# Mixer: the first four heads' attention in two steps with transposes two projected tiles later, and the mLSTM norm's gain as a scale of ScalarE's copies

## The chip, the cores and the metric

The kernel runs on one core of one Trainium2 chip. The metric is the device time of one execution in microseconds (us); of the kernel before there are three runs, with a median of 2618.13 us. One of its executions was recorded by the hardware profiler.

The engines are called by the profile's names: PE (TensorE; PEld is its weight load), DVE (VectorE), ACT (ScalarE), POOL (GpSimd) and SP (the queue that issues most transfers). Each works through its own instructions in order.

## What is computed

One layer of a diffusion backbone over 256 latent and 256 context tokens, width 2048: a half-step FFN, a mixer, a second half-step FFN. The change lies in the mixer, whose normed input `h` is projected by one wide matrix and split:

```
aq, ak, av, mqk, mv, mo, gt = split(h @ w_in)
att = softmax(rope(norm(aq)) @ rope(norm(ak)).T / sqrt(128)) @ av     # 8 heads, 2 key/value heads
hm  = bidirectional mLSTM(mqk, mv, gt)                                # 8 heads of 128
hm  = rms_norm(hm, m_gain) * sigmoid(mo)                              # m_gain: 8 x 128
out = concatenate([att, hm]) @ w_out
```

## The kernel before

All large products are made in three fp32r matmuls: each operand is split into a high and a low part (`split`, L117: ACT copies `hi`, L125; DVE subtracts for `lo`, L126), and `mm3` (L147 to L149) adds hi*hi, hi*lo and lo*hi in PSUM. A weight piece of 1 MB (`raw`, three buffers) is loaded by SP and split into two halves of `hi` and `lo` (four buffers each).

`project(name, n, toks, bs)` multiplies the latents' two token tiles with 512 columns in 16 steps of one k-tile; a step is 2 x 3 matmuls of 128x512 and is called a **projected tile** here. After each step it yields, and the caller may put other work there. So the order on PE is written out by hand: in the loops over `project("w_o1")` and `project("w_q1")` the step number n decides which generator advances: `o_steps` (sigmoid of the output gate into `gm`), `att[0]` (attention of the first four heads), `outs` (norm and gating of `hm`), `cats` (transposes of `hm`). At the end of every step `project` also advances `beside["part"]`: DVE multiplies a 512 KB piece of the modulation weights, already in `sr` (three buffers, loaded by SP, L287), with the condition vector (L205). In w_o1 and w_q1 that is about 1.2 us of DVE per piece, and a buffer is loaded again when its piece is done. The places of all other engines' instructions follow from a scheduler that lists each engine's instructions once, when the program is built.

`attention(kv)` goes over eight items (two query tiles by four heads). Its i-th step does three things:

- item i: scores (3 matmuls), row maximum `nm` (DVE, L1684, L1685), exponential `pr` with its sum `sd` (ACT, L1688), reciprocal (DVE, L1689), scaling of `pr` (ACT, L1690)
- item i-1: four transposes of `pr` on PE (L1696), copied to `pT` (ACT, L1698)
- item i-2: the products of `pT` with the values on PE (L1705)

Called A(i), T(i-1) and V(i-2) here, they stood at one place: steps n = 2, 8, 11, 14 of w_o1 and 2, 5, 8, 11, 14 of w_q1, and the last behind w_q1. T(i) was thus issued with A(i+1), three projected tiles after A(i) (six for i = 0, four for i = 3). Transposes, whether of `pr` or of `hm`, take turns in two PSUM banks (`tr`).

The mLSTM's gain: `m_gain` is loaded once, repeated over all partitions, into `mg` (L1671, SP; its buffer is that of `C1`, which the last mLSTM products, L1523, read). `ev_o` takes the sigmoid into `gm` (ACT, L1625), and POOL multiplies `mg` onto it (L1626). `mlstm_out` multiplies `hm` by `gm` (DVE, L1727) and by the norm's factor (L1728); `mlstm_cat` transposes the 128x128 blocks of `hm` (PE, L1739), and ACT copies each token tile's four blocks at once into `cx` (128x512, L1741).

## Time and profile before

| | |
|---|---|
| runs before (three) | 2616.05, 2618.13, 2618.64 us; median 2618.13 |
| the profiled execution: span, first to last instruction | 2616.0 us |
| the same: what lies around the span | not given; the median is 2.1 us above the span |
| mean granted TensorE clock | 0.998 |
| busy: PE, PEld, DVE, ACT, POOL | 99%, 83%, 80%, 53%, 8% of the span |
| w_o1 and w_q1, steps n = 0 to 15 each | about 1724 to 1790 us in the span |

A row of the timeline gives start, duration, engine, line, operation, and at its end in brackets the idle time of the engine before it with what ended it. Matmuls overlap: one lasts 0.39 us in the row, but the next starts 0.23 us later, so lost time is read from the starts.

### The profile page before, as it was taken

The page shows a single profiled execution, that of the slowest core. Times are in us where ns is not written, and L with a number is a line of the kernel's source. Part 1 is how long each engine was busy: PE and PEld are TensorE (multiplying, and loading weights), DVE is VectorE, ACT ScalarE, POOL GpSimd, SP SyncE. Part 2 cuts the span into 40 slices and gives each one's busy share as a digit, 9 for nine tenths or more (in the row PEclk, how much of TensorE's full clock was granted, in tenths as well). Part 3 has the DMA queues.
Part 4 walks back from the last instruction along what each step waited for, and adds up shares of the span by engine and source line. Part 5 has one row for each costly group of instructions (what it writes and reads, how often), then busy time and mean ns, then how long its engine had stood idle before and what let it go on. Part 6 is the DMA issues. An engine that isn't in the chain of part 4 may idle for free.

```text
span 2616.0 us, 33774 instructions
## 1 busy us (share of the span) xinstructions
PE 2593.1 (99%) x12742; PEld 2159.5 (83%) x12742; DVE 2099.3 (80%) x2792; ACT 1393.4 (53%) x1798; POOL 208.8 (8%) x261
## 2 busy tenths in 40 slices
PE   8999999999999999999999999999999999999998
PEld 5788888888888888888889889878898888888887
DVE  7788888878888788888886889788887676767767
ACT  5455444444444565444454367557576655555554
POOL 0000010100010100000110000220000000000001
PEclk9999999999999999999999999999999999999999
DMA  9889999999999988889986877777769897988875
GB/s 399 347 213 267 281 267 281 256 275 276 277 274 281 265 248 236 226 214 229 230 243 262 311 272 253 240 245 270 248 231 299 261 252 253 253 248 257 242 225 175
DMA packets 126932, 678.93 MB, mean 260 GB/s; under 512 B 14120, under 2 KB 16680, under 8 KB 64944
## 3 DMA queue, kind: packets, MB, share of 16 engines
q1 hardware_dynamic: 99408, 499.54, 51.4%
q0 software_dynamic: 27360, 177.22, 34.9%
q8 instruction: 100, 1.64, 0.2%
q14 instruction: 64, 0.52, 0.1%
HBM read 658.82 MB, written 17.89 MB: 259 GB/s over the span
## 4 chain that ended last, share of the span: by engine, by line
PE 92%; DVE 3%; DMA 3%; issue 1%; ACT 1%; POOL 0%; SPq 0%; ACTq 0%; POOLq 0%; DVEq 0%
PE mm L147 24%; PE mm L149 24%; PE mm L148 24%; PE mm L85 2%; PE tr L148 2%; PE tr L149 2%; PE tr L147 2%; PE Y L149 1%; PE Y L148 1%; PE Y L147 1%; DMA mraw<-in_w_m 1%; PE X L147 1%; PE X L149 1%; PE X L148 1%; PE tr L85 1%; DVE lo L126 1%
## 5 line engine op out<-in xcount | busy, mean ns | idle before, releaser
L125 ACT ACTIVATE hi<-raw 128x1024 fp32r<-128x1024 f32 (+3 forms) x536 | 556.5, 1042 | 579.6 <-PE mm L149 448.8
L126 DVE TENSOR_TENSOR lo<-raw,hi 128x1024 fp32r<-128x1024 f32 (+1 forms) x524 | 630.1, 1208 | 288.2 <-ACT hi L125 268.8
L125 ACT ACTIVATE hi<-chain 128x1024 fp32r<-128x1024 f32 x320 | 338.1, 1060 | 257.3 <-PE mm L149 150.1
L126 DVE TENSOR_TENSOR lo<-chain,hi 128x1024 fp32r<-128x1024 f32 x320 | 386.8, 1221 | 84.4 <-ACT hi L125 80.0
L147 PE MATMUL mm<-hi,hhi 128*128 128x512 f32 (+3 forms) x1024 | 394.6, 385 | 0.0
L148 PE MATMUL mm<-lo,hhi 128*128 128x512 f32 (+3 forms) x1024 | 387.6, 379 | 0.0
L149 PE MATMUL mm<-hi,hlo 128*128 128x512 f32 (+3 forms) x1024 | 387.3, 378 | 0.0
L205 DVE SCALAR_TENSOR_TENSOR junk<-sraw,cBh 128x1024 fp8e5<-128x1024 f32 x192 | 234.4, 1221 | 26.0 <-DMA sraw<-in_w_mt 23.7
L149 PEld LDWEIGHTS mm<-hi,hlo 128*128 128x128 f32 x1024 | 192.9, 188 | 34.0
L147 PEld LDWEIGHTS mm<-hi,hhi 128*128 128x128 f32 x1024 | 192.9, 188 | 31.4
L148 PEld LDWEIGHTS mm<-lo,hhi 128*128 128x128 f32 x1024 | 193.2, 189 | 30.7
L149 PE MATMUL mm<-hi,hid2l 128*128 128x512 f32 x352 | 137.4, 390 | 0.0
L147 PE MATMUL mm<-hi,hid2h 128*128 128x512 f32 x352 | 137.2, 390 | 0.0
L148 PE MATMUL mm<-lo,hid2h 128*128 128x512 f32 x352 | 137.1, 389 | 0.0
L148 PE MATMUL mm<-lo,h2hi 128*128 128x512 f32 x320 | 124.9, 390 | 0.1
L147 PE MATMUL mm<-hi,h2hi 128*128 128x512 f32 x320 | 124.9, 390 | 0.0
L149 PE MATMUL mm<-hi,h2lo 128*128 128x512 f32 x320 | 124.6, 389 | 0.0
L205 DVE SCALAR_TENSOR_TENSOR sr<-sr,cBl 128x1024 f32<-128x1024 f32 x85 | 102.8, 1219 | 14.7 <-DMA sr<-in_w_mt 14.4
L728 POOL DMA_DIRECT2D chain<-in_w_up1b x60 | 53.0, 884 | 725.3 <-DVE lo L126 698.4
L147 PE MATMUL mm<-hhi,hi 128*128 128x512 f32 (+1 forms) x288 | 101.2, 351 | 0.0
L149 PE MATMUL mm<-hhi,lo 128*128 128x512 f32 (+1 forms) x288 | 98.9, 343 | 0.0
L148 PE MATMUL mm<-hlo,hi 128*128 128x512 f32 (+1 forms) x288 | 98.9, 343 | 0.0
(514 smaller groups left out, 5456.3 us busy)
## 6 DMA issues: line engine op xcount, KB each, us to landing
raw<-in_w_dn SPq DMA_DIRECT2D x70, 1024.0 KB, 7.0
chain<-in_w_up1b POOLq DMA_DIRECT2D x60, 1024.0 KB, 10.5
raw<-in_w_up2b SPq DMA_DIRECT2D x50, 1024.0 KB, 5.7
sraw<-in_w_mt SPq DMA_DIRECT2D x96, 512.0 KB, 8.7
sr<-in_w_mt SPq DMA_DIRECT2D x82, 512.0 KB, 5.3
raw<-in_w_up1b SPq DMA_DIRECT2D x40, 1024.0 KB, 8.1
mraw<-in_w_m SPq DMA_DIRECT2D x32, 1024.0 KB, 7.6
chain<-in_w_dn POOLq DMA_DIRECT2D x30, 1024.0 KB, 8.6
```

What stands on the lines that cost most here:

```text
L85: ins = getattr(self.engine, name)(*a, **k)
L125: scalar[0].activation(hi, src, AF.Copy)
L126: vector[0].tensor_tensor(lo, src, hi.bitcast(F32), op=ALU.subtract)
L147: tensor[0].matmul(out_ap, sh, mh, start=first, stop=False, skip_group_check=skip)
L148: tensor[0].matmul(out_ap, sh, ml, start=False, stop=False, skip_group_check=skip)
L149: tensor[0].matmul(out_ap, sl, mh, start=False, stop=last, skip_group_check=skip)
L205: ins = nc.vector.scalar_tensor_tensor(junk() if junk else raw, raw, 1.0, cB[s], op0=ALU.mult, op1=ALU.mult, accum_out=mT[:, i, s, kt, h : ...
L728: accum = lambda dst, src: nc.gpsimd.dma_start(dst, src, accum_op=ALU.add)
```

## The change

1. `attention(kv, apart=False)`: with `apart` it yields between A(i) and T(i-1). `att[0]` is built with it, so T and V have places of their own. In w_o1 the steps are now n = 2 (two), 8, 10, 11, 13, 14; in w_q1 n = 0, 2, 4, 5, 7, 8, 10, 11, 13, 14 (two). The scores stay at 2, 8, 11, 14 and 2, 5, 8, 11. T(0) to T(6) and V(0) to V(5) come two projected tiles later; T(7) with V(6) stays at n = 14 of w_q1, and V(7) behind w_q1. `attention(1)` is unchanged.
2. `mg`, its load and POOL's four multiplications are gone. The gain lies in eight new columns of `vecs` (`mgT`, one per head, along the partitions), and the copy of a turned tile, 128x512, becomes four copies of 128x128, each with its head's column as scale.

```
-    vecs = cst.tile([P, 9 * KT + 3 * KT + 16 * 5 + 16], F32, name="vecs")
+    vecs = cst.tile([P, 9 * KT + 3 * KT + 16 * 5 + 16 + NH], F32, name="vecs")
+    mgT = vecs[:, 288:296]
...
             nc.scalar.activation(o, b, AF.Sigmoid)
-            nc.gpsimd.tensor_tensor(o, o, mg[:, c * 512 : (c + 1) * 512], op=ALU.mult)
...
-        mg = one([P, 1024], "mg", tag="C1")
-        nc.sync.dma_start(mg, I["m_gain"].partition_broadcast(P))
...
-        def attention(kv):
+        def attention(kv, apart=False):
...
                     pr[i] = p
+                if apart:
+                    yield
                 if 0 <= i - 1 < len(items):
...
-                nc.scalar.activation(cxs[c, t], tb, AF.Copy)
+                for g in range(4):
+                    w = slice(g * P, (g + 1) * P)
+                    nc.scalar.activation(cxs[c, t][:, w], tb[:, w], AF.Copy, scale=mgT[:, 4 * c + g : 4 * c + g + 1])
...
-        att = [attention(0), attention(1)]
+        att = [attention(0, True), attention(1)]
...
         for n, _ in enumerate(project("w_o1", 512, (2, 3), bo[1])):
             if n % 4 == 1:
                 steps(o_steps)
-            elif n % 3 == 2:
-                steps(att[0])
+            steps(att[0], {2: 2, 8: 1, 10: 1, 11: 1, 13: 1, 14: 1}.get(n, 0))
...
         for n, _ in enumerate(project("w_q1", 512, (2, 3), bq[1])):
             if n in (1, 4):
                 steps(o_steps)
-            elif n % 3 == 2:
-                steps(att[0])
-            elif n in (6, 9):
+            if n in (6, 9):
                 steps(outs[0])
             elif n in (10, 13):
                 steps(cats[0])
-            elif n in (12, 15):
+            steps(att[0], {0: 1, 2: 1, 4: 1, 5: 1, 7: 1, 8: 1, 10: 1, 11: 1, 13: 1, 14: 2}.get(n, 0))
+            if n in (12, 15):
                 steps(outs[1])
```

The eight columns make `vecs` 32 bytes longer in every partition. Everything allocated behind it on the same side of SBUF starts 32 bytes later in the built program: `raw`, `hi`, `lo` and the chains of weights, which began at multiples of 512 bytes, and `hid2h`, `h2hi` of the second FFN; `hhi`, `sumshh`, `cathi` and others on the other side stay.

The scheduler's lists show the change at three places. Line numbers behind L112 differ by one or two between the kernels. The first place is PE in w_o1 behind A(1), whose last matmul is the first row; `tr<-ident,pr` is T(0). Before:

```order
L149 MATMUL mm<-hhi,hlo 128x512
L1696 MATMUL tr<-ident,pr 128x128 x4
L147 MATMUL mm<-hi,hhi 128x512
L148 MATMUL mm<-lo,hhi 128x512
L149 MATMUL mm<-hi,hlo 128x512
```

The same place on PE now, down to T(0):

```order
L150 MATMUL mm<-hhi,hlo 128x512
L148 MATMUL mm<-hi,hhi 128x512
L149 MATMUL mm<-lo,hhi 128x512
L150 MATMUL mm<-hi,hlo 128x512
L148 MATMUL mm<-hi,hhi 128x512
L149 MATMUL mm<-lo,hhi 128x512
L150 MATMUL mm<-hi,hlo 128x512
L148 MATMUL mm<-hi,hhi 128x512
L149 MATMUL mm<-lo,hhi 128x512
L150 MATMUL mm<-hi,hlo 128x512
L148 MATMUL mm<-hi,hhi 128x512
L149 MATMUL mm<-lo,hhi 128x512
```

T(0) stood right behind A(1); now 12 matmuls, two projected tiles, stand between them (one more, L150, follows the last row shown).

The second place is DVE around the reciprocal `sd` of item 1, which ACT needs for the scaling of `pr` (1). Before:

```order
L205 SCALAR_TENSOR_TENSOR sr_10852,mT<-sr_10852,cBl 128x1024
L1685 TENSOR_SCALAR nm<-nm 128x1
L205 SCALAR_TENSOR_TENSOR sr_10853,mT<-sr_10853,cBl 128x1024
L126 TENSOR_TENSOR lo<-raw,hi 128x1024
L1689 RECIPROCAL sd<-sd 128x1
```

The same place on DVE now:

```order
L206 SCALAR_TENSOR_TENSOR sr_10852,mT<-sr_10852,cBl 128x1024
L1684 TENSOR_SCALAR nm<-nm 128x1
L206 SCALAR_TENSOR_TENSOR sr_10853,mT<-sr_10853,cBl 128x1024
L1688 RECIPROCAL sd<-sd 128x1
L206 SCALAR_TENSOR_TENSOR sr_10851,mT<-sr_10851,cBl 128x1024
```

A split of weights (`lo`) stood ahead of the reciprocal and now stands behind it.

The third place is DVE at the end of w_q1, around items 6 and 7: from the reciprocal `sd` of item 6 to that of item 7. Before:

```order
L1689 RECIPROCAL sd<-sd 128x1
L205 SCALAR_TENSOR_TENSOR sr_10853,mT<-sr_10853,cBl 128x1024
L205 SCALAR_TENSOR_TENSOR sr_10851,mT<-sr_10851,cBl 128x1024
L126 TENSOR_TENSOR lo<-raw,hi 128x1024
L1684 TENSOR_REDUCE nm<-mm 128x1
L126 TENSOR_TENSOR lo<-raw,hi 128x1024
L1685 TENSOR_SCALAR nm<-nm 128x1
L205 SCALAR_TENSOR_TENSOR sr_10851,mT<-sr_10851,cBl 128x1024
L1689 RECIPROCAL sd<-sd 128x1
```

The same place now, from the piece ahead of the reciprocal of item 6:

```order
L206 SCALAR_TENSOR_TENSOR sr_10851,mT<-sr_10851,cBl 128x1024
L1688 RECIPROCAL sd<-sd 128x1
L206 SCALAR_TENSOR_TENSOR sr_10853,mT<-sr_10853,cBl 128x1024
L127 TENSOR_TENSOR lo<-raw,hi 128x1024
L206 SCALAR_TENSOR_TENSOR sr_10851,mT<-sr_10851,cBl 128x1024
L1683 TENSOR_REDUCE nm<-mm 128x1
L127 TENSOR_TENSOR lo<-raw,hi 128x1024
L1684 TENSOR_SCALAR nm<-nm 128x1
L1688 RECIPROCAL sd<-sd 128x1
```

The last two pieces that come through the buffer `sr_10851` moved up: the second of them stood between the maximum `nm` of item 7 and its reciprocal, and now stands ahead of the maximum.

More of the change, by code (lines that the diff above doesn't have):

```diff
@@ L2321, in _laid_out @@
         "gate_b": asc(a["gate_b"][0]),
-        "m_gain": asc(a["m_gain"][0]),
         "q_gain": asc(a["q_gain"][0]),
@@ L2328, in _laid_out @@
     cw = a["conv_w"][0].T.reshape(16, P, 5).transpose(1, 0, 2).reshape(P, 80)
-    m["vecs"] = asc(np.concatenate([part(a["b_mod"][0]), part(a["g_norm"][0]), cw, part(a["conv_b"][0])], 1))
+    m["vecs"] = asc(np.concatenate([part(a["b_mod"][0]), part(a["g_norm"][0]), cw, part(a["conv_b"][0]), part(a["m_gain"][0])], 1))
     wm = a["w_mod"][0].reshape(D, 9, D)
```

## The prediction

> **What bounds the kernel.** I first read the page's busy line, then who waited for whom on PE over the whole span.

> ```profile
> PE 2593.1 (99%) x12742; PEld 2159.5 (83%) x12742; DVE 2099.3 (80%) x2792; ACT 1393.4 (53%) x1798; POOL 208.8 (8%) x261
> PE tr L1696 <- ACT pr L1690: 3.2, 2, 2.3
> PE tr L464 <- ACT cc L188: 2.8, 1, 2.8
> PE tr L85 <- DMA mraw<-in_w_m: 2.7, 3, 1.3
> ```

> PE is the bound: it is idle for 23 us of 2616. The longest entry (us in total, times, longest) is the change's place: twice, transposes of `pr` waited for ACT's scaling. Nothing the change does removes PE work, so it can bring only what PE loses there, and take what it makes PE lose elsewhere. PE's timeline gives the loss.

> ```profile
> 1738.28 0.39 PE L149 MATMUL mm<-hhi,hlo 128*128 128x512 f32 x1
> 1739.56 0.65 PE L1696 MATMUL tr<-ident,pr 128*128 128x128 f32 x4 [0.89 <-ACT pr L1690]
> ...
> 1744.85 0.38 PE L1705 MATMUL mm<-pT,av 128*128 128x128 f32 x2
> 1747.49 0.66 PE L1696 MATMUL tr<-ident,pr 128*128 128x128 f32 x4 [2.26 <-ACT pr L1690]
> 1747.98 0.91 PE L1705 MATMUL mm<-pT,av 128*128 128x128 f32 x6
> 1748.57 0.75 PE L147 MATMUL mm<-hi,hhi 128*128 128x512 f32 x1
> ...
> 1752.07 0.39 PE L149 MATMUL mm<-hi,hlo 128*128 128x512 f32 x1
> ...
> 1754.84 0.40 PE L149 MATMUL mm<-hhi,hlo 128*128 128x512 f32 x1
> 1755.08 0.60 PE L1696 MATMUL tr<-ident,pr 128*128 128x128 f32 x4
> 1755.51 1.06 PE L1705 MATMUL mm<-pT,av 128*128 128x128 f32 x8
> 1756.33 0.48 PE L147 MATMUL mm<-hi,hhi 128*128 128x512 f32 x1
> 1756.64 0.40 PE L148 MATMUL mm<-lo,hhi 128*128 128x512 f32 x1
> 1749.00:1750.00 1.00, 1.00 (x4) 0.71 (x4) 0.70 (x2) 0.26 (x1) 0.00 (x0) 0.50 1.01 274
> ```

> The group at 1754.84 shows the undisturbed pace, start to start: 0.24 us from the last score matmul to its transposes, 0.82 for eight products (two per item in the first rows would take 0.21), 0.31 for the first 512-wide matmul, then 0.23 each. Against it:

> - T(0): 1739.56 - 1738.28 = 1.28, less 0.24: **1.04 us lost**.
> - T(1): 1747.49 - 1744.85 = 2.64, less 0.21: **2.43 lost**.
> - From 1748.57 to 1752.07 eight matmuls start in 3.50 us, not in 0.31 + 7 x 0.23 = 1.92; the transposes before took 0.49, not 0.43: **1.64 lost**. The window row has the reason: its granted clock (third number from the end) is 0.50.

> Together 5.11 us. All else in these two projections runs at PE's pace.

> **Why `pr` was late.** DVE's timeline, with the scaling on ACT:

> ```profile
> 1729.34 0.69 DVE L1727 TENSOR_TENSOR hm<-hm,gm 128x512 f32<-128x512 f32 x1 [2.85 <-POOL gm L1626]
> ...
> 1734.46 0.68 DVE L1684 TENSOR_REDUCE nm<-mm 128x1 f32<-128x512 f32 x1
> ...
> 1738.60 0.15 DVE L1689 RECIPROCAL sd<-sd 128x1 f32<-128x1 f32 x1
> ...
> 1744.24 1.23 DVE L205 SCALAR_TENSOR_TENSOR sr<-sr,cBl 128x1024 f32<-128x1024 f32 x1 [0.71 <-DMA sr<-in_w_mt]
> 1745.39 1.22 DVE L126 TENSOR_TENSOR lo<-raw,hi 128x1024 fp32r<-128x1024 f32 x1
> 1746.52 0.15 DVE L1689 RECIPROCAL sd<-sd 128x1 f32<-128x1 f32 x1
> 1746.71 0.72 ACT L1690 ACTIVATE pr<-pr,sd 128x512 f32<-128x512 f32 x1 [2.31 <-DVE sd L1689]
> ```

> DVE stood 2.85 us for POOL's gain, so everything behind was late. Later the reciprocal of item 1 stood behind a piece that waited 0.71 us for its load, and behind a split of 1.13 us.

> **Part 1, the transposes.** T(0) is now due two tiles (12 x 0.228 = 2.74 us) later, at 1738.5 + 2.7 = 1741.2; `pr` (0) was complete at 1739.5 even with DVE's wait. The wait goes, with 1.7 us to spare. T(1) is due at 1746.55 (1738.5, two tiles, T(0) 0.43, a tile and scores 2.1, two tiles). `pr` (1) was complete at 1746.71 + 0.72 = 1747.43. The split that moved behind its reciprocal takes 1.13 off: 1746.3. This alone leaves only 0.25 us.

> **Part 2, POOL's gain.** Without DVE's wait, the first row above starts at 1726.5. Between nothing and 2.85 us of that reaches item 1, since the scores come only at 1738.5; the pieces' reloads also start earlier. So `pr` (1) has 0.25 to 3.1 us to spare; I take both waits as gone, and with them the half clock, which began behind the longer of them: **-5.11**. (Behind the shorter, 1.04 us, the next matmuls start at full pace.) POOL's own time was beside PE's and counts nothing. SP loses one load of 512 KB and a wait:

> ```profile
> SPq L1671 <- PE tr L1523: 6.5, 1, 6.5
> L1530 ACT ACTIVATE hm<-tr,den x16: 342/352/370, 1597.0 to 1708.8; 128x128 f32<-128x128 f32 x16
> L1741 ACT ACTIVATE cx<-tr x4: 576/582/600, 1779.6 to 1796.0; 128x512 f32<-128x512 f32 x4
> 1780.00:1790.00 10.00, 10.00 (x60) 8.42 (x59) 5.06 (x8) 5.56 (x10) 0.00 (x0) 1.00 0.82 304
> 1790.00:1800.00 10.00, 10.00 (x52) 8.19 (x51) 9.60 (x15) 8.59 (x13) 2.11 (x3) 1.00 0.92 341
> 1797.96 1.06 ACT L125 ACTIVATE hi<-raw 128x1024 fp32r<-128x1024 f32 x1 [0.28 <-PE mm L149]
> ```

> Loads behind `mg` on SP can start up to 6.5 us earlier; PE waited for none of them: 0. Each copy of a turned tile becomes four scaled ones; the nearest row is a scaled 128x128 copy out of PSUM, 352 ns, so 1.41 us for 0.58, +0.83 us of ACT, four times. Two fall where ACT is busy 5.6 of 10 us (fourth busy value), two where it is busy 8.6: there 1.4 us of idle ACT must take 1.7. The last row is one of ACT's splits there: it waited for PE to free its buffer, so the splits are ahead of PE, and I cost this at nothing; uncovered it would be 0.3 us, at most 1.7.

> **What is late next: T(7).** It stays at its place, and before it was met by 0.06 us:

> ```profile
> 1785.33 1.23 DVE L205 SCALAR_TENSOR_TENSOR sr<-sr,cBl 128x1024 f32<-128x1024 f32 x1 [1.73 <-DMA sr<-in_w_mt]
> 1786.48 0.16 DVE L1689 RECIPROCAL sd<-sd 128x1 f32<-128x1 f32 x1
> 1786.67 0.72 ACT L1690 ACTIVATE pr<-pr,sd 128x512 f32<-128x512 f32 x1 [2.26 <-DVE sd L1689]
> 1787.45 0.66 PE L1696 MATMUL tr<-ident,pr 128*128 128x128 f32 x4
> sr<-in_w_mt SPq DMA_DIRECT2D x1, 512.0 KB, 3.2
> sr<-in_w_mt SPq DMA_DIRECT2D x1, 512.0 KB, 5.8
> ```

> In the changed order T(7) is due at 1787.45 - 5.1 = 1782.35, and the last two pieces through `sr_10851` now stand ahead of the maximum of item 7, each behind its own reload. The last two rows are these reloads before: 3.2 us, and 5.8 with 1.5 MB asked for just ahead. Walking the new DVE order from the previous piece (ends 1768.0): reload, with 3.2 us, lands 1771.3; piece 1.15, to 1772.5; next reload, 3.2 to 5.8, lands 1775.8 to 1778.4; piece, maximum 0.6, split 1.14, `nm` 0.1: 1778.8 to 1781.4; exponential 0.8; two of `cx`'s copies 0.6; `pr` 0.7; two more copies 0.6, since T(7) uses the bank that they empty: 1781.5 to 1784.1. T(7) waits between 0 and 1.8 us. Before the second reload now goes one load of 1 MB, 3.4 us earlier, which is the case of the 3.2 us row; but two loads of `late` come right behind. I take **+0.5**, a wait too short for the clock to fall.

> **The sum** on the profiled execution: 2616.0 - 5.1 + 0.5 = 2611.4. The median lies 2.1 us above its span: **2613.5**, 0.18% below 2618.13. About 0.2% (5.2 us) is what a measurement of this kernel can tell from no change; the forecast lies at the edge of it.

> [...] The granted clock fell to 0.50 about 0.9 us after a gap of 2.4 us. [...] **Rival: the half clock stays**, bound to the stretch and not to the wait: 2613.5 + 1.6 = 2615.1. The rows speak against it: the 0.50 begins right behind the gap, and the same products ran at full clock before. 7%.

> **Rival: T(7) takes the gain back.** With 5.8 us for both reloads the first lands 2.6 later, and the second with it: a wait of 1.8 + 2.6 = 4.4, and behind so long a gap the half clock, 1.6: 2613.5 - 0.5 + 6.0 = 2619.0. For it: both reloads stand in DVE's order with 2.4 us of other work between. Against it: little is asked for ahead of the first. 13%.

> **Rival: the change doesn't do what it says.** If item 1 stays late by 1.9 us, since its reloads are no earlier, PE waits at T(1) for that and little of the clock's loss goes: 2613.5 + 3.5 = 2617. For it: 0.25 us is all that Part 1 alone leaves. Against: DVE's 2.85. 7%.

> **Rival on the other side: the 32 bytes.** The tiles moved by `vecs` are read by PE all through the second FFN.

> ```profile
> L147 PE MATMUL mm<-hi,hid2h 128*128 128x512 f32 x352 | 137.2, 390 | 0.0
> L147 PE MATMUL mm<-hi,h2hi 128*128 128x512 f32 x320 | 124.9, 390 | 0.0
> 10.00:60.00 50.00, 47.17 (x409) 31.45 (x402) 38.27 (x88) 27.47 (x59) 2.70 (x4) 1.00 1.01 425
> L1522 PE MATMUL tr<-v1l,E x96: 272/275/275, 1589.4 to 1704.7; 128*128 128x130 f32 x96
> ```

> With their two sisters each, 3 x 352 + 3 x 320 = 2016 matmuls, at 0.228 us 460 us of PE, stream a moved tile. If a stream from a start that is 32 bytes off were 3% longer (7 ns), that would be 14 us: 2628, slower. It decides from 2.1%, 9.7 us. The nearest row streams 130 columns at steps of 520 bytes, and takes 275 ns beside 273 for 128-wide transposes: nothing to 0.7%, under 3.3 us. 10%. The same shift under loads: from 10 to 60 us the DMA engines are busy 1.01 of the time at 425 GB/s, so each 1% longer load is 0.5 us. [...]

> **How the numbers follow.** The forecast (both waits gone, T(7) within 1.8 us) has 58%, the rivals 7, 13, 7 and 10%, and 5% are left for a gain that I don't see. Low end: no wait at T(7) (2613.0), less 1.5 for the spread of the runs and a gain of 0.5 elsewhere: 2611.0. High end: it takes in 2615.1, 2617 and most of 2619.0: 2618.5; what is left out is mainly the 10% above. Faster by over 0.2% is below 2612.9: 0.6 us under the forecast, inside the runs' spread of 2.6: 0.42 of 58%, and the 5%: 0.30. Slower: 0.10. Within: 0.60.

> **What would show it.** In the changed profile: no wait of T(0) and T(1) for `pr`, the granted clock at 1.00 from 1740 to 1760, DVE's wait for POOL at `hm` gone; each step right if so. T(7) with a wait of 0 to 1.8 us, with DVE's maximum of item 7 behind a piece that waits for its load. PE's undisturbed matmuls in the second FFN still at 390 ns. Wrong: new waits of PE behind 1785 for `cathi` or `hi`, longer matmuls anywhere, or loads that land later in the first 60 us.

## The result, and the profile after

| | us |
|---|---|
| before, four runs | 2616.05 to 2619.84, median 2618.39 |
| after, four runs | 2654.10 to 2656.69, median 2655.05 |
| ratio | 1.014, 95% interval 1.0126 to 1.0155 |
| profiled execution after | span 2653.0 (before 2616.0), clock 0.996 (before 0.998) |

The change costs 36.7 us, where 4.6 were to be gained. The page after: its busy line, and the list of what PE waited for (us in total, times, longest):

```profile
PE 2629.9 (99%) x12742; PEld 2155.8 (81%) x12742; DVE 2103.8 (79%) x2792; ACT 1395.3 (53%) x1810; POOL 203.1 (8%) x257
```

```profile
PE tr L85 <- DMA mraw<-in_w_m: 3.6, 3, 2.3
PE tr L465 <- ACT cc L189: 2.9, 1, 2.9
...
PE tr L1697 <- ACT cx L1744: 0.8, 1, 0.8
```

The transposes' waits for `pr`, 3.2 us, are gone, and T(7) now waits 0.8 us. PE is idle for 23 us, as before. So PE is *busy* for 37 us longer with the same 12742 matmuls, and no list of waits can show where. The view by stage can: of before, then of after, the stretches from 140 to 1350 us (first FFN) and from 1990 to 2600 us (second FFN); behind each engine's busy time stands the number of its instructions.

```profile
140.00:1350.00 1210.00, 1209.56 (x5408) 999.11 (x5407) 1007.67 (x1213) 599.89 (x670) 120.72 (x137) 1.00 0.94 255
...
1990.00:2600.00 610.00, 610.00 (x2729) 504.42 (x2728) 434.32 (x437) 338.03 (x356) 39.16 (x45) 1.00 0.84 246
```

```profile
140.00:1350.00 1210.00, 1209.90 (x5274) 973.55 (x5273) 988.11 (x1180) 586.35 (x644) 116.50 (x132) 1.00 0.93 248
...
1990.00:2600.00 610.00, 609.92 (x2716) 501.53 (x2715) 433.51 (x424) 344.78 (x360) 34.36 (x40) 1.00 0.85 252
```

In the first FFN PE starts 5274 matmuls where it started 5408, at full clock (third number from the end) and with under 0.5 us of idle time: each takes 2.5% longer on average. 1210 x 5408 / 5274 - 1210 = 30.7 us of the 36.7 are lost there, 370 us and more ahead of the code that was changed. In the second FFN it is 0.5%. The groups by line and shape say which matmuls: of before, then of after (the first name behind the arrow is the operand that streams, the second the stationary one; then count, busy us, mean ns).

```profile
L147 PE MATMUL mm<-hi,n1h 128*128 128x512 f32 x160 | 62.2, 389 | 0.0
...
L147 PE MATMUL mm<-hi,hhi 128*128 128x256 f32 x64 | 18.3, 287 | 0.0
```

```profile
L148 PE MATMUL mm<-hi,h2hi 128*128 128x512 f32 x320 | 124.8, 390 | 0.0
...
L148 PE MATMUL mm<-hi,n1h 128*128 128x512 f32 x160 | 63.2, 395 | 0.0
...
L148 PE MATMUL mm<-hi,hhi 128*128 128x256 f32 x64 | 18.1, 283 | 0.0
```

`hi` moved by 32 bytes in all three. With `h2hi`, which moved with it, the matmul lasts 390 ns as before; with `n1h`, which stayed, 395 in place of 389. From start to start, in the trace's nanoseconds, the median of the 7464 512-wide matmuls with one operand on each side of SBUF goes from 227 to 234. From their starts to the next matmul's it is 1732.3 us in sum before and 1772.7 after (40.4 us); for the 2375 with both operands on the left 540.9 and 541.4. Streams of 256 columns did not get longer (287 and 283 ns).

### The profile page after: what moved, and what is told of

Read it like the earlier page. It is cut to its first block, busy times and chain, and to the rows that moved or that the text cites. A ratio compares the mean times of both kernels' runs of the same rounds, so it can differ in the third digit from the quotient of the medians.

```text
span 2653.0 us, 33782 instructions
## 1 busy us (share of the span) xinstructions
PE 2629.9 (99%) x12742; PEld 2155.8 (81%) x12742; DVE 2103.8 (79%) x2792; ACT 1395.3 (53%) x1810; POOL 203.1 (8%) x257
## 3 DMA queue, kind: packets, MB, share of 16 engines
q8 instruction: 100, 1.64, 0.2%
## 4 chain that ended last, share of the span: by engine, by line
PE 93%; DVE 3%; DMA 2%; ACT 1%; issue 1%; POOL 0%; ACTq 0%; POOLq 0%; DVEq 0%
PE mm L148 25%; PE mm L150 25%; PE mm L149 25%; PE mm L85 3%; PE tr L150 2%; PE tr L148 2%; PE tr L149 2%; PE Y L149 1%; PE Y L148 1%; PE Y L150 1%; PE tr L85 1%; PE X L148 1%; PE X L149 1%; PE X L150 1%; DVE lo L127 1%
## 5 line engine op out<-in xcount | busy, mean ns | idle before, releaser
L126 ACT ACTIVATE hi<-raw 128x1024 fp32r<-128x1024 f32 (+3 forms) x536 | 556.6, 1042 | 598.2 <-PE mm L150 488.9
L126 ACT ACTIVATE hi<-chain 128x1024 fp32r<-128x1024 f32 x320 | 338.9, 1061 | 268.9 <-PE mm L150 174.8
L148 PE MATMUL mm<-hi,hhi 128*128 128x512 f32 (+3 forms) x1024 | 396.9, 388 | 0.0
L149 PE MATMUL mm<-lo,hhi 128*128 128x512 f32 (+3 forms) x1024 | 390.6, 381 | 0.0
L150 PE MATMUL mm<-hi,hlo 128*128 128x512 f32 (+3 forms) x1024 | 390.5, 381 | 0.0
L150 PEld LDWEIGHTS mm<-hi,hlo 128*128 128x128 f32 x1024 | 192.0, 188 | 37.8
L148 PEld LDWEIGHTS mm<-hi,hhi 128*128 128x128 f32 x1024 | 192.2, 188 | 35.5
L149 PEld LDWEIGHTS mm<-lo,hhi 128*128 128x128 f32 x1024 | 192.4, 188 | 34.9
L150 PE MATMUL mm<-hi,hid2l 128*128 128x512 f32 x352 | 137.6, 391 | 0.0
L148 PE MATMUL mm<-hi,hid2h 128*128 128x512 f32 x352 | 137.3, 390 | 0.0
L149 PE MATMUL mm<-lo,hid2h 128*128 128x512 f32 x352 | 137.2, 390 | 0.0
L149 PE MATMUL mm<-lo,h2hi 128*128 128x512 f32 x320 | 124.8, 390 | 0.1
L148 PE MATMUL mm<-hi,h2hi 128*128 128x512 f32 x320 | 124.8, 390 | 0.0
L150 PE MATMUL mm<-hi,h2lo 128*128 128x512 f32 x320 | 124.8, 390 | 0.0
L148 PE MATMUL mm<-hhi,hi 128*128 128x512 f32 (+1 forms) x288 | 101.8, 354 | 0.0
L149 PE MATMUL mm<-hlo,hi 128*128 128x512 f32 (+1 forms) x288 | 99.6, 346 | 0.0
L150 PE MATMUL mm<-hhi,lo 128*128 128x512 f32 (+1 forms) x288 | 99.5, 346 | 0.0
## 6 DMA issues: line engine op xcount, KB each, us to landing
sraw<-in_w_mt SPq DMA_DIRECT2D x96, 512.0 KB, 7.9
sr<-in_w_mt SPq DMA_DIRECT2D x82, 512.0 KB, 5.6
```

What stands on the lines that cost most here:

```text
L126: scalar[0].activation(hi, src, AF.Copy)
L148: tensor[0].matmul(out_ap, sh, mh, start=first, stop=False, skip_group_check=skip)
L149: tensor[0].matmul(out_ap, sh, ml, start=False, stop=False, skip_group_check=skip)
L150: tensor[0].matmul(out_ap, sl, mh, start=False, stop=last, skip_group_check=skip)
```

## The experiments

**Who moved against whom.** Theory: the 32 bytes cost PE its step. Theory A: what counts is how a matmul's two operands stand to each other; theory B: a start 32 bytes off is slow by itself. Rival: the order or the missing load did it. Four kernels move the left side, the right side, both or none.

`e1_after_old_places`, the change with all weight buffers where they were:

```diff
 # of the changed kernel
-    cst.tile([P, 48], F32, name="cstpad")
+    cst.tile([P, 40], F32, name="cstpad")
```

> The changed kernel, whole, with the filler tile behind the vectors 32 bytes shorter, so that every weight buffer starts where it did before. Theory (the 32 bytes cost PE its step): 512-wide matmuls are back at 227 ns from start to start in the first FFN, and what is left is the gain forecast for the two parts, 2618.4 - 5.1 + 0.5 to 0.8: 2613 to 2615. Rival (the changed order or the removed load does it, the addresses are innocent): 2655, and 234 ns from start to start as in the changed kernel.

`e2_before_left_32`, no part of the change, only the move:

```diff
 # of the kernel before
-    cst.tile([P, 48], F32, name="cstpad")
+    cst.tile([P, 56], F32, name="cstpad")
```

> The kernel before, with nothing of the change but the filler tile 32 bytes longer: weight buffers (hi, lo, raw, chains) start 32 bytes past a multiple of 64, the other side's operands stay. Theory: some 7250 undisturbed 512-wide matmuls that stream an operand of the other side take about 5.8 ns more each, 42 us: 2618 + 42 = 2660, and the second FFN's products with hid2h and h2hi, which move along, stay at 227 ns. Rival (order): 2618.

`e3_after_both_32`, the change with the right side moved along, and `e4_before_right_32`, the kernel before with the right side alone moved:

```diff
 # of the changed kernel (e3), of the kernel before (e4)
-    edge.tile([P, 56], F32, name="edge")
+    edge.tile([P, 48], F32, name="edge")
```

> The changed kernel with its weight buffers 32 bytes past, as built, and the other side's tiles (hhi, sumshh, n1h, cathi) moved 32 bytes in the same direction, so that stationary and moving rows stand to each other as before. Theory A (what counts is how the two operands of a matmul stand to each other): 227 ns, 2613 to 2615. Theory B (a weight row or a load's target that starts 32 bytes past a multiple of 64 is slow by itself): still 234 ns, 2655. What the first 60 us lose with 227 ns back is the loads' share.

> The kernel before with only the other side's tiles (hhi, sumshh, n1h, cathi) moved by 32 bytes; weight buffers, loads and chains start where they did. Theory A (relation of the two operands): slow as with the weights moved, 234 ns and about 2655 to 2660. Theory B (weights or loads by their own start): 227 ns and 2618.

| | left moved | right moved | median us | ratio to before (median 2619.32), 95% |
|---|---|---|---|---|
| e1 (changed) | no | no | 2616.76 | 0.9997, 0.9985 to 1.0008 |
| e2 (before) | 32 | no | 2658.84 | 1.0148, 1.0133 to 1.0164 |
| e3 (changed) | 32 | 32 | 2617.43 | 0.9992, 0.9983 to 1.0001 |
| e4 (before) | no | 32 | 2658.82 | 1.0148, 1.0131 to 1.0165 |

The same group in e1, e2, e3 and e4:

```profile
L148 PE MATMUL mm<-hi,n1h 128*128 128x512 f32 x160 | 62.2, 389 | 0.0
```

```profile
L147 PE MATMUL mm<-hi,n1h 128*128 128x512 f32 x160 | 63.2, 395 | 0.0
```

```profile
L148 PE MATMUL mm<-hi,n1h 128*128 128x512 f32 x160 | 62.2, 389 | 0.0
```

```profile
L147 PE MATMUL mm<-hi,n1h 128*128 128x512 f32 x160 | 63.3, 396 | 0.0
```

(The ratio is of all runs; e1's reach from 2614.28 to 2629.18, and the slowest is the profiled one. The intervals of e1 and e3 take in 1, and both lie 2 us above the 2613 to 2615 expected.) Theory A holds, B and the rival fall. e2 carries no line of the change's work and loses 39.5 us; e4 leaves every weight, load and chain in place and loses the same; e3 has both operands 32 bytes off and loses nothing. The two effects add up: 39.5 lost (e2) less 2.6 gained (e1) is 36.9, measured 36.7.

**How far, and which load.** `e8_before_left_64` has 64 in place of 48 in `cstpad`; `e10_before_right_128` and `e11_before_right_96` have 24 and 32 in place of 56 in `edge`, all in the kernel before.

> The kernel before with the weight buffers moved by 64 bytes instead of 32, the other side's tiles as they were. If the two operands' starts must agree modulo 64 bytes: 227 ns, about 2618. If any move against each other costs (or a multiple of 128 or 512 is needed): 234 ns, about 2659.

> The kernel before with the other side's tiles moved by 128 bytes. Known so far, as the distance of the two operands' starts modulo 256: 0 gives 227 ns, 32 either way 234, 64 one way 226 to 232. If the pattern repeats every 128 bytes: 227 and about 2619. If it repeats every 256 bytes only, 128 is the far end: something from 227 to 234 and 2620 to 2659.

> The kernel before with the other side's tiles moved by 96 bytes. If the pattern repeats every 128 bytes, this is 32 from a good place: 231 to 234 ns and about 2659. If an odd multiple of 32 is what costs: the same. If the cost falls off with distance: nearer to 229 ns and 2630.

One run each: 2631.89 us (64), 2658.48 (128), 2662.92 (96), beside 2619.46 for before's median in the first case and one run of 2622.54 in the others. At 128 and 96 bytes the steps have medians of 232 and 234 ns. At 64 it depends on the place in the triple; its three groups with `n1h` and `n1l`:

```profile
L147 PE MATMUL mm<-hi,n1h 128*128 128x512 f32 x160 | 62.9, 393 | 0.0
L149 PE MATMUL mm<-hi,n1l 128*128 128x512 f32 x160 | 62.8, 392 | 0.0
L148 PE MATMUL mm<-lo,n1h 128*128 128x512 f32 x160 | 62.1, 388 | 0.0
```

The 64 bytes came out between the two values expected, 2618 and 2659. So neither "any multiple of 64" nor "every 128" holds. By the built program's addresses, which no trace shows, the two operands' starts are 0 (`h2hi`) or 256 bytes (`n1h` before) apart, modulo 512, where the pace is full; since 32, 64, 96 and 128 bytes off that are slower, the pattern does not repeat every 128 bytes or less. What lies between (from start to start 226 to 232 ns at 64, 232 at 128, 234 at 32 and 96) follows no simple distance.

A product is three matmuls, a triple: `hi` streams past `hhi`, `lo` past `hhi`, `hi` past `hlo`. While one streams, the next one's stationary operand is loaded: in the trace that load starts 3 ns behind the stream's start (the median, in all kernels). `e9_one_operand` moves `hlo` and leaves `hhi`, `e12_moving_lo` moves `lo` (and the load buffers) and leaves `hi`:

```diff
 # e9, of the kernel before
-    edge.tile([P, 56], F32, name="edge")
+    edge.tile([P, 40], F32, name="edge")
...
     hhi = hpool.tile([P, KT, 512], F32R, tag="hh", name="hhi")
+    hpool.tile([P, 8], F32, name="hpad", bufs=1)
     hlo = hpool.tile([P, KT, 512], F32R, tag="hl", name="hlo")
+    hpool.tile([P, 8], F32, name="hpad2", bufs=1)
...
 # e12, of the kernel before
+    pads = []
...
-    sm.tile([P, 16], F32, name="smpad", bufs=1)
+    sm.tile([P, 8], F32, name="smpad", bufs=1)
...
+                    if tag == "lo" and not pads:
+                        pads.append(wp.tile([P, 8], F32, name="lopad", bufs=1))
                     m = wp.tile([P, 1024], F32R, tag=tag, name=tag, bufs=4)[:32]
```

> The kernel before with hlo alone moved by 32 bytes against hhi, hi and lo (sumshl, which takes its place in the first FFN, moves with it). Each product's three matmuls go hhi x hi, hhi x lo, hlo x hi, the first named being the stationary operand. Theory N (a matmul's stream is disturbed by the weight load of the NEXT matmul, which runs beside it): the matmul hhi x lo, which has hlo's load beside it, goes from 227 to 234 ns, and hlo x hi stays. Theory O (a matmul's stream against its OWN weights): hlo x hi goes to 234 ns, hhi x lo stays. In either case products whose weights all come from sumshl are slow, and the sum is about 720 x 6 + 832 x 6 ns = 9 us above before's 2619.

> The kernel before with lo (and the load buffers raw behind it) moved by 32 bytes; hi and all stationary operands stay. In the triple hhi x hi, hhi x lo, hlo x hi, only the middle matmul now streams from 32 past a good place. Theory N (a stream against the weight load that runs beside it): the middle one alone is slow, from 227 to 234 ns or as high as 239, the two others stay at 227 to 228; this holds in the second FFN too, where it did not get slower before. Rival (any operand out of step slows the whole triple, as the two slow matmuls with hlo moved suggest): two or three of the triple above 231 ns. Sum by N with 7 ns: 3300 middle matmuls, 23 us, 2642; with 12 ns 2659.

One run each: 2641.96 us (before 2622.54) and 2660.67 (before 2618.38). The three groups with `hhi` and `hlo` of before and of e9, then those with `n1h` and with `h2hi` of e12:

```profile
L147 PE MATMUL mm<-hi,hhi 128*128 128x512 f32 x832 | 332.0, 399 | 0.0
L148 PE MATMUL mm<-lo,hhi 128*128 128x512 f32 x832 | 325.3, 391 | 0.0
L149 PE MATMUL mm<-hi,hlo 128*128 128x512 f32 x832 | 325.2, 391 | 0.0
```

```profile
L147 PE MATMUL mm<-hi,hhi 128*128 128x512 f32 x832 | 334.4, 402 | 0.0
L148 PE MATMUL mm<-lo,hhi 128*128 128x512 f32 x832 | 332.5, 400 | 0.0
L149 PE MATMUL mm<-hi,hlo 128*128 128x512 f32 x832 | 324.4, 390 | 0.0
```

```profile
L150 PE MATMUL mm<-lo,h2hi 128*128 128x512 f32 x320 | 127.7, 399 | 0.0
L149 PE MATMUL mm<-hi,h2hi 128*128 128x512 f32 x320 | 126.4, 395 | 0.0
L151 PE MATMUL mm<-hi,h2lo 128*128 128x512 f32 x320 | 125.1, 391 | 0.0
...
L150 PE MATMUL mm<-lo,n1h 128*128 128x512 f32 x160 | 63.6, 398 | 0.0
L149 PE MATMUL mm<-hi,n1h 128*128 128x512 f32 x160 | 62.9, 393 | 0.0
L151 PE MATMUL mm<-hi,n1l 128*128 128x512 f32 x160 | 62.2, 388 | 0.0
```

The middle one lengthens most in both, 400 for 391 and 398 for 389 ns: the only one whose stream is out of step with the load beside it. In e9 the last one streams past weights that moved, and keeps its pace, 390 for 391: its own weights don't count there (theory O falls). Theory N has the right place but not the whole size: the middle one loses 12 (e9) and 10 ns (e12) from start to start, not 7, and the first of the triple, in step with the load beside it, loses 6 and 4. The medians of the triple add up to 700 ns in e9 and 694 in e12, where N with 7 ns has 688. Why the neighbour slows is open. In e12 the products of the second FFN with `h2hi` and `hid2h`, at 227 ns in every other kernel, have the same pattern. e9 lost 19 us, not the 9 expected, and not from these triples alone: its groups with `sumshl`, with `cathi` and `catlo`, and with `n1f`, `s2f`, `s3f` and `s4f` step at 232 to 235 ns too, so it moved more than `hlo`. The reading rests on the groups with `hhi` and `hlo`, and on e12.

Beside a load that is out of step a stream of 512 columns lasts 6 to 9 ns longer (395 for 389 in the changed kernel, 400 for 391 in e9, 398 for 389 in e12), and 9839 of this kernel's 12742 matmuls (the 7464 and 2375 above) are streams of 512 columns.

**The two parts, each alone, at the old places.** `e5_order_alone` is the kernel before with the first item of the diff and none of the second (`mg` and POOL's gain stay); `e6_gain_alone` is e1 with the loops over w_o1 and w_q1, and `att[0]`, as before the change.

> The kernel before with the first part of the change alone: attention in two steps, transposes two projected tiles later; POOL keeps its gain, all tiles stay where they were. Theory of the prediction (the first part takes away T(0)'s wait and leaves T(1) with 0.25 us to spare): no wait of T(0), at most a short one of T(1), clock 1.00 there; about 5 us gained in w_o1 and w_q1, less what T(7) loses to its late reload (1 to 5 us seen with both parts): 2615 to 2618 against about 2619 before. Rival (the second part, not the first, freed DVE): T(1) still waits 1 to 2 us and the sum is 2617 to 2619.

> The second part alone at the old places: the gain as the scale of the copies, the old order of the attention. If DVE's wait for POOL was what made the scaled probabilities late, T(0) and T(1) lose less than the 1.0 and 2.4 us of before: 2615 to 2617. If the transposes' place decides, both waits stay at 1 and 2 us with the half clock behind, and the sum is 2619, within 1 us.

`e7_reload_elsewhere` is e1 with one number of the table that paces DVE's pieces (the 107th piece, from the 163rd step to the 165th):

```diff
-PACE += (83, 102), (87, 109), (91, 118), (94, 130), (97, 144), (101, 152), (107, 163), (110, 170), (128, 181)
+PACE += (83, 102), (87, 109), (91, 118), (94, 130), (97, 144), (101, 152), (107, 165), (110, 170), (128, 181)
```

> The changed kernel at the old places with one number of the pieces' pace table moved (the 107th piece two steps later), so that the pieces ahead of item 7's maximum come through three buffers by turns and none waits for a reload asked for just before. Theory (DVE's wait for this reload is what makes T(7) late): DVE's 3 to 4 us wait for a piece ahead of the maximum goes, T(7) waits under 0.5 us, and the whole gain is left: 2618.7 - 5 = 2613 to 2614.5. Rival (ACT's four scaled copies, which T(7)'s bank waits for, make it late): T(7) still waits 1 to 2 us, 2616 to 2617.

| | median us, 11 runs | ratio to before (2619.46), 95% | 8300th to 8900th matmul, us |
|---|---|---|---|
| before | | | 120.9 |
| e5, order alone | 2621.36 | 1.0009, 1.0000 to 1.0018 | 123.2 |
| e6, gain alone | 2616.61 | 0.9990, 0.9981 to 0.9998 | 119.9 |
| e1, e3, both | (above) | (above) | 120.7, 117.7 |
| e7, both, reload elsewhere | 2614.69 | 0.9983, 0.9974 to 0.9992 | 115.7 |

The last column is the time between the same two matmuls in the profiled execution: from some 50 us ahead of w_o1 to behind V(7). By the medians part 1 alone loses 1.9 us (2615 to 2618 were expected), and part 2 alone gains 2.9, no less than both parts at the old places (2.6 and 1.9): the new order shows no gain on balance until e7. e6's profiled execution, 2619.15 us, lies 2.5 above its median, so its trace shows 1.0 us of the gain only. e5's PE timeline at T(1), T(4) and T(7), its ACT's at the scaling of `pr` (1), its DVE's and its POOL's ahead of T(4):

```profile
1747.44 0.60 PE L1698 MATMUL tr<-ident,pr 128*128 128x128 f32 x4
...
1769.00 0.65 PE L1698 MATMUL tr<-ident,pr 128*128 128x128 f32 x4 [1.65 <-ACT pr L1690]
...
1788.08 1.12 PE L1698 MATMUL tr<-ident,pr 128*128 128x128 f32 x4 [3.01 <-ACT pr L1690]
```

```profile
1746.43 0.73 ACT L1690 ACTIVATE pr<-pr,sd 128x512 f32<-128x512 f32 x1 [0.60 <-DVE sd L1689]
```

```profile
1740.21 2.46 DVE L126 TENSOR_TENSOR lo<-raw,hi 128x1024 fp32r<-128x1024 f32 x2
...
1763.59 3.38 DVE L126 TENSOR_TENSOR lo<-raw,hi 128x1024 fp32r<-128x1024 f32 x2
```

```profile
1762.59 2.16 POOL L1626 TENSOR_TENSOR gm<-gm,mg 128x512 f32<-128x512 f32 x1 [5.22 <-ACT gm L1625]
```

Part 1 alone does free T(0) and T(1): `pr` (1) is complete at 1746.43 + 0.73 = 1747.16, 0.28 us ahead of T(1). It loses the gain again at T(4) and T(7). At T(4) POOL's gain has a hand in it: two splits of DVE that run while POOL multiplies take 3.38 us, and 2.46 elsewhere. With part 2 (e1, e3, e7) T(4) does not wait. Part 2 alone frees T(0), which no longer waits (120.9 - 119.9 = 1.0 us), and leaves T(1) late: e6's PE timeline there.

```profile
1748.46 0.66 PE L1697 MATMUL tr<-ident,pr 128*128 128x128 f32 x4 [2.20 <-ACT pr L1689]
```

T(7) with both parts: DVE's last piece ahead of item 7's maximum, ACT's scaling of `pr` (7) and the copies behind it, and T(7), all in e3; then T(7) in e1 with DVE's last piece there; then DVE's last piece in the changed kernel as built; then the same stretch of DVE in e7.

```profile
1781.79 1.23 DVE L206 SCALAR_TENSOR_TENSOR sr<-sr,cBl 128x1024 f32<-128x1024 f32 x1 [3.83 <-DMA sr<-in_w_mt]
```

```profile
1786.09 0.73 ACT L1689 ACTIVATE pr<-pr,sd 128x512 f32<-128x512 f32 x1
1786.70 0.63 ACT L1744 ACTIVATE cx<-tr,vecs 128x128 f32<-128x128 f32 x2
```

```profile
1787.38 0.66 PE L1697 MATMUL tr<-ident,pr 128*128 128x128 f32 x4 [1.79 <-ACT cx L1744]
```

```profile
1796.70 0.87 PE L1697 MATMUL tr<-ident,pr 128*128 128x128 f32 x4 [3.26 <-ACT cx L1744]
```

```profile
1791.10 1.23 DVE L206 SCALAR_TENSOR_TENSOR sr<-sr,cBl 128x1024 f32<-128x1024 f32 x1 [3.96 <-DMA sr<-in_w_mt]
```

```profile
1813.45 1.22 DVE L206 SCALAR_TENSOR_TENSOR sr<-sr,cBl 128x1024 f32<-128x1024 f32 x1 [2.91 <-DMA sr<-in_w_mt]
```

```profile
1776.01 1.21 DVE L206 SCALAR_TENSOR_TENSOR sr<-sr,cBl 128x1024 f32<-128x1024 f32 x1
...
1779.09 0.69 DVE L1683 TENSOR_REDUCE nm<-mm 128x1 f32<-128x512 f32 x1 [0.73 <-PE mm L150]
```

In e3 DVE stands 3.83 us for the reload, in e1 3.96, in the changed kernel 2.91, and T(7) waits 1.8, 3.3 and 0.8 us (in e1 with half clock behind, 0.50 from 1797 to 1798 us). The e1 shown is its slowest execution, 12.4 us above its median; most of that is lost at 472 and 963 us, behind waits of 2.4 and 1.9 us for DVE with half clock behind, both far ahead of the changed code. In e7 the piece ahead of the maximum finds its data there, the maximum waits only for PE, and T(7) does not wait. So the reload is the cause; the copies of `cx` only stand last in the chain, and where they do they add 0.5 us (e3: `pr` (7) is complete at 1786.82, the copies at 1787.33, and T(7) starts). e7 is faster than both kernels: 4.8 us under before's median, its interval clear of 1.

## Why the prediction was wrong, point by point

- **What bounds the kernel.** PE does; right. But "takes what it makes PE lose elsewhere" was looked for in waits, while what came is busy time.
- **T(0), T(1) and the half clock, -5.11.** Right with both parts: no wait, clock 1.00, and 120.9 - 115.7 = 5.2 us where nothing else is late (e7). (Before, the clock fell 1.1 us behind the gap's end, 1748.61 - 1747.49, where 0.9 was read.) The 0.25 us that part 1 alone leaves at T(1) came out as 0.28 (e5). The credit to part 2 was misplaced: DVE's wait for POOL is not what T(1) needs gone (e6: it still waits 2.2 us). Its going frees T(0), which part 1 frees as well, and with part 1 it helps T(4).
- **POOL's own time "counts nothing".** Wrong where its multiplication lies beside DVE's splits: two splits took 0.92 us longer there (e5), so with both parts its going is a gain.
- **T(7), +0.5.** The mechanism was right, link by link; the size wasn't: 0.8 us in the changed kernel, 1.8 in e3, 3.3 and the half clock in e1. The forecast took the reloads nearer to the short end; DVE waits 2.9 to 4.0 us for the last. The rival "T(7) takes the gain back" happened in the profiled execution of e1. e7, without the wait, gains 4.8 us where e1 and e3 gain about 2: the difference fits a late T(7), though only the profiled executions show it.
- **`cx`'s four copies, 0.** Right unless T(7) is late; then 0.5 us.
- **The failed step is "Rival on the other side: the 32 bytes".** It stood at nothing in the sum of 2613.5 us, and it is what happened. Its price for a slow stream, 3% or 7 ns, came out as supposed (227 to 234 ns), which was luck, as no row had shown it. Three things in it were wrong. It counted the 2016 matmuls of the second FFN, "tiles moved by `vecs`", and just those stayed at 390 ns, since both their operands moved; it left out that `hi` and `lo`, moved too, stream in nearly all the others, where the stationary operand stayed: 7464 matmuls, 40 us. It took a start for good or bad by itself, and not against the operand that is read beside it. And it gave 10% on a row of 130-column streams, which could not speak for 512: streams of 256 columns got no longer either (287 and 283 ns).
- **The same shift under loads.** At most small: 1000 matmuls behind the first, PE is at 136.6 to 137.2 us where the whole left side is 32 bytes off (after, e2, e3) or 64 (e8), and at 134.9 to 136.3 where it stays (before, e1, e4 to e7, e9 to e11) and in e12 (135.2), which by its edit moves `raw` but not the load buffer `mraw`. No run isolates the loads' share, and the groups lie only 0.3 us apart.

## What to carry to other kernels

A small tile ahead of others is an edit to every address behind it. List what moves and what stays, and for each matmul-heavy stage ask whether its streamed and its stationary operand still stand to each other as before; if not, a filler of the right size can undo it, as in e1 and e3 (2616.76 and 2617.43 us for 2655.05). And when the time grows without waits, count instructions per stretch at equal clock: the page's list of waits is blind to it. A transfer that an engine waits for is judged by the place in *that engine's* order where the wait falls; e7 took it away with one number.

- By the median, a matmul of 512 columns starts 227 ns behind the one before it when the two sides' operands stand to each other as before the change, 232 when they are 128 bytes off that (e10), 234 at 32 (after) and 96 (e11), and 226 to 232 at 64, by the place in the triple (e8); with both 32 bytes off, the group with `n1h` takes 389 ns as before (e3). In e9 and e12 the one of a triple that lengthens most is that whose stream is out of step with the stationary operand loaded beside it: 400 for 391 and 398 for 389 ns.
- Beside POOL's multiplication of two SBUF tiles two DVE subtractions took 3.38 us, and two elsewhere 2.46 (e5). In the kernel before, one that started 0.22 us behind POOL's, at 1732.23, took 2.30 us where others take 1.22; one that started 0.36 us ahead of POOL's, at 1755.01 in e5, kept its 1.22. What makes the difference was not shown.
- The clock fell behind gaps between matmuls' starts of 2.2 (e4, e12), 2.5 (before, e6) and 3.6 us (e1), and not behind 2.2 (e3), 2.5 (e2) and 2.8 (e9): the gap's length alone does not decide it. What fits these traces better is how long PE was busy in stretches of 3.413 us: in each trace the clock's changes are whole multiples of that apart (in the kernel before, the fall at 1748.61 is 504 of them behind the change at 28.29). Of the stretches counted off so between 60 and 2600 us, ten end with a fall to half clock, and in them PE was busy for 0.30 to 1.68 us of 3.41; in all others that ran at full clock it was busy for 1.70 or more, but for one (e11, 1.58). Two such stretches, from before (a fall at its end) and from e9 (none; its gap of 2.8 us began in the stretch ahead):

```profile
1745.20:1748.61 3.41, 1.15 (x12) 1.12 (x11) 3.41 (x8) 1.90 (x3) 0.00 (x0) 1.00 0.95 336
```

```profile
1764.89:1768.30 3.41, 1.73 (x13) 1.64 (x14) 3.41 (x6) 2.15 (x3) 0.00 (x0) 1.00 1.00 351
```
